# A float32 decoder block on one core: gate weights loaded into later tiles of the mixer, the row factor built a unit sooner, one opening cast behind the root

## The chip, the core and the metric

The kernel runs on one core of a Trainium2 chip. The engines of the core are called here as the profile calls them: PE (TensorE, matrix products), DVE (VectorE), ACT (ScalarE), POOL (GpSimd) and SP (SyncE, which issues nearly all DMA loads here). The metric is the device time of one execution in microseconds (us); a lower time is better.

## The reference

One layer of a decoder block on x of 256 tokens by 2048 columns, all in float32: a half-step feed-forward, a mixer of two head groups, a second half-step feed-forward, and a last norm.

```python
def rms_norm(x, gain):
    xf = x.astype(jnp.float32)
    var = jnp.mean(xf * xf, axis=-1, keepdims=True)
    return (xf * lax.rsqrt(var + NORM_EPS) * gain.astype(jnp.float32)).astype(x.dtype)

def swiglu_ffn(x, w_gate, w_up, w_down):
    return (jax.nn.silu(x @ w_gate) * (x @ w_up)) @ w_down
...
        x = x + FFN_RESIDUAL_SCALE * swiglu_ffn(rms_norm(x, ffn1_norm[l]),
                                                ffn1_w_gate[l], ffn1_w_up[l], ffn1_w_down[l])
        z = rms_norm(x, mix_norm[l]) @ w_in[l]
        ...
        xc = causal_depthwise_conv(lru_x, lru_conv_w[l]) + lru_conv_b[l]
        h = rg_lru(xc, lru_w_a[l], lru_b_a[l], lru_w_i[l], lru_b_i[l], lru_lambda[l])
        y_lru = h * jax.nn.gelu(lru_gate, approximate=True)
        y_sc = sc_b * causal_depthwise_conv(sc_c * sc_x, sc_conv_w[l])
        y = jnp.concatenate([rms_norm(y_lru, lru_out_norm[l]),
                             rms_norm(y_sc, sc_out_norm[l])], axis=-1)
        x = x + y @ w_out[l]
```

The feed-forward is 5632 wide, `w_in` has 5120 columns, and the gates of `rg_lru` are eight blocks of 128 by 128 in `lru_w_a` and in `lru_w_i`.

## The kernel before

**Products in parts.** A float32 operand is split into a high part `hi` (a cast on ACT) and a rest `lo` (a subtraction on DVE), and a product is made of hi by hi, lo by hi and hi by lo. Weights come in units of 512 rows by 512 columns (1 MB, a tile `raw_...`). `load` (line 165) issues the DMA on SP, `parts_of` makes two ACT casts of 128x1024 and one DVE subtraction of 128x2048. The pool `raws` has three raw buffers, which are used in turn: a load can go out when the subtraction has let go of the buffer three units back. The pool `splits` has two hi and two lo buffers; a cast waits until PE has left the unit two back. Every engine, and SP's queue too, works in order. Nearly all instructions are recorded through one helper, so they carry its line, 43.

**The mixer.** `columns` multiplies w_in, 512 columns at a time, in four units (u = 0 to 3) into four banks `ps_in`: per unit 16 matmuls with hi (512 columns wide) and 16 with lo (256 wide). A bank is one of eight of the PSUM pool. The normed x is turned into `xT_nm`, a tile for each unit, without the row factor 1/sqrt(mean of squares); that is multiplied in afterwards. `Norm.factor` makes it from the sums of squares (tiles `tot`, `v`, `s`, `y`, `q`, `r`), and `Norm.rows` spreads it: two diagonal tiles on DVE, two matmuls with ones into the bank `pb_nm`, and a DVE copy to `bc_nm`. The list `order` runs ten blocks of columns; the first two are `lru_x`. Behind the first block stand the row factor, then `gate_weights`, called twice: it loads the eight gate blocks (512 KB) into a buffer of `raws` (`rawgate_a`, `rawgate_i`), casts them and subtracts. In the names of the first block's tiles, `in_0_2` is unit 2 of block 0 and `in_1_0` unit 0 of the second block. `lru_x` then adds the two halves of each bank, multiplies by `bc_nm` to `zx`, and leaves the convolution (`xc`), its split (`xs`) and the gate products (`pgate_a`, `pgate_i`) to be issued between later units.

**Tiles of the mixer.** `tmp` takes tiles by tag from the pool `mixw`. The tags `d` and `v` have one buffer each of 128x1024. Their first user is the end of the first block's recurrence, many units later. The pool stands where the first feed-forward had its `keep` tiles, the last of which hold the crossed columns `cross_nm`; ACT reads those last.

**The opening.** `begin` is written out by hand and keeps its order (`Engine.pinned`). It multiplies the first units of the gate and up weights while x still arrives in four column groups (`load_x`). On ACT: two quarters of the up unit's cast at once (`hi_u_start`), the third quarter, the last square of the norm (`junk_n`), the root (`s_n`), the fourth quarter, then the tokens `n`. On DVE the chain from the sum `tot_n` over the root to `r_n`, then `lo_u_start`, the scaling of `ps_g`, and so on. `root`, made at the very start, loads the table for the square root.

A scheduler orders the instructions that are not pinned, so the order on each engine is read from the built program below.

Of the kernel before, what the change touches and what calls it, by code (L numbers as in the profile page):

```python
# [10 lines left out]
F32 = mybir.dt.float32  # L11
# [6 lines left out]
P = 128  # L18
D = 2048
# [5 lines left out]
CW = 512  # L25
NC_D = D // CW
UK = 4
NH = 8
# [21 lines left out]
def hybrid_block(ctx: ExitStack, tc: tile.TileContext, a: dict, out: bass.AP):  # L50
    nc = tc.nc
    Engine.pinned = False
    dve, act, pe = (Engine(tc, e) for e in (nc.vector, nc.scalar, nc.tensor))
# [6 lines left out]
    def defer(cost, fn):  # L60
        pending.append((cost, fn))

    def flush():
        while pending:
            pending.popleft()[1]()

    def pump(budget):

        owed[0] = min(owed[0], 0.0) + budget
        while pending and owed[0] > 0:  # L70
            cost, fn = pending.popleft()
            fn()
            owed[0] -= cost
# [5 lines left out]
    raws = ctx.enter_context(tc.tile_pool(name="raws", bufs=3, side="right"))  # L79
# [3 lines left out]
    def bank(name):  # L83
        return psum.tile([P, 512], F32, tag="ps", name=name)

    def f32(ap):
        return ap.bitcast(F32)
# [62 lines left out]
    def big(name):  # L150

        return bigs.tile([P, UK, 2 * S], F32R, tag="big", name=name)
# [39 lines left out]
    def unit(src, name):  # L192
        return parts_of(load(src, name), name)
# [21 lines left out]
    def onward():  # L215

        if moving:
            two, _, fn = moving.popleft()
            fn(two)
        if tasks:  # L220
            key, begin, fn = tasks.popleft()
            moving.append((begin(), key, fn))

    def on_the_way():
        return {task[0] for task in tasks} | {entry[1] for entry in moving}
# [103 lines left out]

    def columns(w, c0, xT, name):
        ps = [bank(f"ps_{name}_{f}") for f in range(4)]
        for u in range(KD // UK):
            blk = unit(w[u * UK * P : (u + 1) * UK * P, c0 : c0 + CW], f"{name}_{u}")
            assert ("nm", u) not in on_the_way()
            for half in range(2):
                for j in range(UK):
                    x = xT[u][:, j, :]
                    for f in range(4):  # L340
                        wf = blk[j][half][:, f * P : (f + 1) * P]
                        if half == 0:
                            pe.matmul(ps[f], wf, x, start=u == 0 and j == 0, stop=False)
                        else:
                            end = u == KD // UK - 1 and j == UK - 1
                            pe.matmul(ps[f][:, :S], wf, x[:, :S], start=False, stop=end)
            onward()
            pump(1.5)
        return ps

    def product(w, c, us, y, name):
        ps = [bank(f"ps_{name}_{t}") for t in range(NT)]
        cs = slice(c * CW, (c + 1) * CW)
        for i, u in enumerate(us):
            blk = unit(w[u * UK * P : (u + 1) * UK * P, cs], f"{name}_{u}")
            multiply([(ps[t], stationary(y(u), t), i == 0, i == len(us) - 1) for t in range(NT)], blk)
            pump(1.5)
        return ps  # L360
# [110 lines left out]
    def ffn(tag, norm, after, opening=False):  # L471
        with (
# [67 lines left out]
            ps = {(m, t): bank(f"ps_{m}{tag}_0_{t}") for m in "gu" for t in range(NT)}  # L540
            ws = {"g": wg, "u": wu}

            def first_columns(m, u, **how):
                return load(ws[m][u * UK * P : (u + 1) * UK * P, :CW], f"{m}{tag}_0_{u}", **how)

            def begin():
# [4 lines left out]
                raw = {("g", 0): first_columns("g", 0, pieces=pieces)}  # L551
# [58 lines left out]
                units.extend(big(f"x{tag}_{u}") for u in range(4))  # L610
                ru, (hi, lo, blk) = raw["u", 0], splits_of("u_start")
                act.copy(hi[:, :2], ru[:, :2])
                act.copy(hi[:, 2:3], ru[:, 2:3])
                norm.squares(3, (dve, act), lambda: pair[:, 0])
                norm.factor()
                act.copy(hi[:, 3:], ru[:, 3:])
                dve.tensor_tensor(lo, ru, f32(hi), op=ALU.subtract)
                n = tokens(1)
                rows = [stationary(norm.xT[0], t) for t in range(NT)]
# [231 lines left out]
    nm = held["nm"]  # L851


    with tc.tile_pool(name="mixer", bufs=1) as mp, tc.tile_pool(name="mixw", bufs=2) as mw:
        wgate = {}

        def gate_weights(key, src):
            raw = raws.tile([P, NH, P], F32, tag="raw", name=f"rawgate_{key}")
            nc.sync.dma_start(raw, src.rearrange("h i j -> i h j"))
            both = bigs.tile([P, 2, NH, P], F32R, tag="big", name=f"gate_{key}")  # L860
            hi, lo = both[:, 0], both[:, 1]
            act.copy(hi, raw)
            dve.tensor_tensor(lo, raw, f32(hi), op=ALU.subtract)
            wgate[key] = (hi, lo)
# [4 lines left out]
        w_in = a["w_in"][0]  # L869
# [3 lines left out]
        def tmp(tag, name, w=S, dt=F32, bufs=2):  # L873
            return mw.tile([P, w], dt, tag=tag, name=f"{tag}_{name}", bufs=bufs)
# [61 lines left out]
        def finish(y, k, gain, grp, first):  # L936
            sq = tmp("ysq", k)
            act.activation(sq, y, AF.Square)
            ac = acc[:, grp, :]
            if first:  # L940
                dve.tensor_copy(ac, sq)
            else:
                dve.tensor_tensor(ac, ac, sq, op=ALU.add)
            hi, lo = yT[k // UK][:, k % UK, :S], yT[k // UK][:, k % UK, S:]
            act.activation(hi, y, AF.Copy, scale=gain)
            dve.scalar_tensor_tensor(lo, y, gain, f32(hi), op0=ALU.mult, op1=ALU.subtract)
# [73 lines left out]
        def sc_b(ps, half):  # L1020
            if any(4 * half + f not in ys for f in range(4)):
                flush()
            for f in range(4):
# [4 lines left out]
                dve.tensor_tensor(y, b, y, op=ALU.mult)  # L1028
                defer(0.8, lambda q=q, y=y: finish(y, NH + q, vec["sc_out_norm"][:, q : q + 1], 1, q == 0))

        order = [
            (lru_x, 0, 0), (lru_x, 0, 1), (sc_c, 3, 0), (lru_gate, 1, 0), (sc_x, 4, 0),
            (lru_gate, 1, 1), (sc_c, 3, 1), (sc_x, 4, 1), (sc_b, 2, 0), (sc_b, 2, 1),
        ]
        for i, (use, piece, half) in enumerate(order):
            ps = columns(w_in, piece * (D // 2) + half * CW, nm.xT, f"in_{piece}_{half}")
            if i == 0:
                flush()
                nm.factor()
                nm.rows(lambda name: tmp("half", name, bufs=4))  # L1040
                bc = nm.bc
                dve.tensor_tensor(bc2, bc, bc, op=ALU.mult)
                gate_weights("a", a["lru_w_a"][0])
                gate_weights("i", a["lru_w_i"][0])
                yT += [big(f"yT_{u}") for u in range(KD // UK)]
            use(ps, half)

# [4 lines left out]
        for c in range(NC_D):  # L1052
            cs = slice(c * CW, (c + 1) * CW)
            for g in range(2):
                if c == 0 and g == 1:
                    flush()
                ps = product(w_out, c, (2 * g, 2 * g + 1), yT.__getitem__, f"o{c}_{g}")
# [92 lines left out]
```

## Time and profile before

| | |
|---|---|
| median of 3 runs | 1722.84 us (1720.89 to 1723.07) |
| the profiled execution, whole | 1723.02 us |
| its span, first to last instruction | 1721.2 us |
| mean granted PE clock in the span | 0.997 |
| DMA, mean over the span | 208 GB/s |
| loads of w_in, each 1 MB, median to landing | 5.1 us |

The profile is of one execution, so sums are made against 1723.02. Busy time is summed for each engine; idle time of an engine other than the one that bounds costs nothing. PE's matmuls overlap in their records, so the time of a unit is read from start to start. The text of the next section names views: the page, the waits (who waited for whom), the chain of work that ended last, the timeline, the table by windows, and the DMA issues.

### The profile page before, as it was taken

To read this page: it belongs to the slowest core of one execution; us is meant where nothing else is said; L and a number is where in the kernel's file an instruction comes from. 1 tells how busy PE (TensorE), PEld (TensorE's weight loads), DVE (VectorE), ACT (ScalarE), POOL (GpSimd) and SP (SyncE) were. 2 spreads that over 40 slices of the span, in tenths; PEclk is the share of its full clock that TensorE was granted. 3 is DMA by queue.
4 is the path that set the end of the run, shared out by engine and by line. 5 is a ranking of instruction groups with operands and counts; after the bars stand their busy time and mean duration, and the time that the engine had idled before them with its cause. 6 is when DMAs were issued, how large, how long until landed. Compare 5 with 4: busy or idle time off the path is not lost.

```text
span 1721.2 us, 20206 instructions
## 1 busy us (share of the span) xinstructions
PE 1700.1 (99%) x7811; PEld 1413.6 (82%) x7811; DVE 1477.9 (86%) x1286; ACT 1166.3 (68%) x1481; POOL 6.9 (0%) x32
## 2 busy tenths in 40 slices
PE   8999999999999999999999999999999999999997
PEld 6888888888887887888888888888888888887886
DVE  7988999989889878687987679989989888889796
ACT  6767667676568678765765776786667675677864
POOL 1000000000000000000000000000000000000000
PEclk9999999999999999999999999999999999999999
DMA  8667567585567685746555674585677656566853
GB/s 296 204 212 207 195 220 217 198 280 178 180 215 226 213 250 144 236 155 207 174 191 179 218 262 153 198 268 195 208 218 225 208 192 223 196 214 202 249 192 122
DMA packets 233056, 357.91 MB, mean 208 GB/s; under 512 B 64772, under 2 KB 67200, under 8 KB 232832
## 3 DMA queue, kind: packets, MB, share of 16 engines
q1 hardware_dynamic: 232496, 355.50, 63.9%
q8 instruction: 61, 1.00, 0.2%
q10 hardware_dynamic: 144, 1.05, 0.2%
q14 instruction: 35, 0.29, 0.0%
q0 software_dynamic: 320, 0.07, 0.0%
HBM read 339.82 MB, written 2.10 MB: 199 GB/s over the span
## 4 chain that ended last, share of the span: by engine, by line
PE 88%; DVE 4%; ACT 3%; DMA 2%; issue 2%; SPq 0%; DVEq 0%; ACTq 0%
PE ps_d L43 13%; PE ps_in L43 12%; PE ps_u_a L43 8%; PE ps_g_a L43 8%; PE ps_u_c L43 6%; PE ps_g_c L43 6%; PE ps_o L43 5%; PE ps_d_a L43 5%; PE ps_g_d L43 4%; PE ps_u_d L43 3%; PE ps_g_e L43 3%; PE ps_u_e L43 3%; PE ps_d_c L43 3%; PE ps_d_d L43 2%; PE ps_u L43 2%
## 5 line engine op out<-in xcount | busy, mean ns | idle before, releaser
L43 DVE TENSOR_TENSOR lo_u_p<-raw_u,hi_u_p 128x2048 fp32r<-128x2048 f32 (+1 forms) x80 | 160.0, 2019 | 18.7 <-ACT hi_u_p L43 18.2
L43 ACT CAST hi_u_p<-raw_u 128x1024 fp32r<-128x1024 f32 x140 | 141.6, 1048 | 48.9 <-PE ps_u_a L43 14.7
L43 ACT CAST hi_g_p<-raw_g 128x1024 fp32r<-128x1024 f32 x132 | 133.9, 1047 | 59.2 <-DVE raw_g L43 24.2
L43 PE MATMUL ps_d<-hi_d,h 128*128 128x512 f32 x704 | 167.0, 389 | 0.0
L43 DVE TENSOR_TENSOR lo_g_p<-raw_g,hi_g_p 128x2048 fp32r<-128x2048 f32 (+1 forms) x75 | 151.2, 2031 | 17.3 <-ACT hi_g_p L43 16.8
L43 PE MATMUL ps_in<-xT_nm,hi_in 128*128 128x512 f32 x640 | 154.5, 393 | 2.7 <-DVE bc_nm L43 2.7
L43 PEld LDWEIGHTS ps_d<-hi_d,h 128*128 128x128 f32 x704 | 132.1, 188 | 27.4
L43 PEld LDWEIGHTS ps_in<-xT_nm,hi_in 128*128 128x128 f32 x640 | 118.0, 189 | 26.3 <-DVE bc_nm L43 3.2
L43 ACT CAST hi_d_p<-raw_d 128x1024 fp32r<-128x1024 f32 x84 | 86.1, 1048 | 68.1 <-DVE raw_d L43 24.4
L43 DVE TENSOR_TENSOR lo_d<-raw_d,hi_d 128x2048 fp32r<-128x2048 f32 x44 | 100.2, 2289 | 32.9 <-ACT hi_d L43 32.7
L43 DVE TENSOR_TENSOR lo_in<-raw_in,hi_in 128x2048 fp32r<-128x2048 f32 x40 | 91.4, 2286 | 34.5 <-ACT hi_in L43 33.1
L43 ACT CAST hi_in<-raw_in 128x1024 fp32r<-128x1024 f32 x80 | 80.1, 1046 | 59.4 <-PE ps_in L43 38.8
L43 ACT CAST hi_u_x<-raw_u 128x1024 fp32r<-128x1024 f32 x80 | 81.3, 1047 | 41.8 <-PE ps_u_c L43 28.8
L43 DVE TENSOR_TENSOR lo_d_p<-raw_d,hi_d_p 128x2048 fp32r<-128x2048 f32 (+1 forms) x48 | 96.5, 2020 | 12.3 <-ACT hi_d_p L43 12.0
L43 DVE TENSOR_TENSOR raw_u<-raw_u,raw_u 128x2048 f32<-128x2048 f32 (+1 forms) x50 | 92.3, 1862 | 11.6 <-DMA raw_u<-in_ffn_w_up_dram 11.0
L43 ACT CAST hi_d<-raw_d 128x1024 fp32r<-128x1024 f32 x88 | 88.9, 1045 | 18.9 <-PE ps_d_d L43 7.6
L43 ACT CAST hi_g_x<-raw_g 128x1024 fp32r<-128x1024 f32 x80 | 81.6, 1045 | 28.3 <-PE ps_g_c L43 11.5
L43 DVE TENSOR_TENSOR lo_g_x<-raw_g,hi_g_x 128x2048 fp32r<-128x2048 f32 x40 | 91.4, 2286 | 5.6 <-ACT hi_g_x L43 5.6
L43 DVE TENSOR_TENSOR lo_u_x<-raw_u,hi_u_x 128x2048 fp32r<-128x2048 f32 x40 | 91.4, 2284 | 1.9 <-ACT hi_u_x L43 1.7
L43 DVE TENSOR_TENSOR raw_g<-raw_g,raw_g 128x2048 f32<-128x2048 f32 (+1 forms) x46 | 85.0, 1867 | 6.3 <-DMA raw_g<-in_ffn_w_gate_dram 6.2
L43 PE MATMUL ps_d<-lo_d,h 128*128 128x512 f32 x352 | 87.3, 389 | 0.0
L43 PEld LDWEIGHTS ps_in<-xT_nm,lo_in 128*128 128x128 f32 x640 | 82.5, 192 | 3.2
(399 smaller groups left out, 3671.5 us busy)
## 6 DMA issues: line engine op xcount, KB each, us to landing
raw_d<-in_ffn_w_down_dram SPq DMA_DIRECT2D x88, 1024.0 KB, 5.6
raw_u<-in_ffn_w_up_dram SPq DMA_DIRECT2D x87, 1024.0 KB, 5.3
raw_g<-in_ffn_w_gate_dram SPq DMA_DIRECT2D x86, 1024.0 KB, 5.4
raw_in<-in_w_in_dram SPq DMA_DIRECT2D x40, 1024.0 KB, 5.1
raw_o<-in_w_out_dram SPq DMA_DIRECT2D x16, 1024.0 KB, 5.1
xres<-in_x_dram SPq DMA_DIRECT2D x4, 512.0 KB, 7.5
raw_u<-in_ffn_w_up_dram SPq DMA_DIRECT2D x2, 512.0 KB, 9.2
raw_g_first<-in_ffn_w_gate_dram SPq DMA_DIRECT2D x1, 1024.0 KB, 11.9
```

The costliest lines, as they stand in the source:

```text
L43: ins = getattr(self.engine, name)(*args, **kwargs)
```

## The change

The gate weights are loaded into the tiles `d` and `v` instead of raw buffers; the row factor is made behind unit 1 of the first block and spread behind unit 2, through a callback of `columns`; in the opening, the third quarter of the cast goes behind the root, next to the fourth.

```diff
-    def columns(w, c0, xT, name):
+    def columns(w, c0, xT, name, between=None):
...
             onward()
             pump(1.5)
+            if between:
+                between(u)
         return ps
...
                 act.copy(hi[:, :2], ru[:, :2])
-                act.copy(hi[:, 2:3], ru[:, 2:3])
                 norm.squares(3, (dve, act), lambda: pair[:, 0])
                 norm.factor()
-                act.copy(hi[:, 3:], ru[:, 3:])
+                for j in (2, 3):
+                    act.copy(hi[:, j : j + 1], ru[:, j : j + 1])
...
-        def gate_weights(key, src):
-            raw = raws.tile([P, NH, P], F32, tag="raw", name=f"rawgate_{key}")
+        def gate_weights(key, src, room):
+            raw = tmp(room, f"gate_{key}", NH * P, bufs=1).rearrange("p (h j) -> p h j", h=NH)
...
+        def row_factor(u):
+            if u == 1:
+                flush()
+                nm.factor()
+            elif u == 2:
+                nm.rows(lambda name: tmp("half", name, bufs=4))
+
...
-            ps = columns(w_in, piece * (D // 2) + half * CW, nm.xT, f"in_{piece}_{half}")
+            between = row_factor if i == 0 else None
+            ps = columns(w_in, piece * (D // 2) + half * CW, nm.xT, f"in_{piece}_{half}", between)
             if i == 0:
-                flush()
-                nm.factor()
-                nm.rows(lambda name: tmp("half", name, bufs=4))
                 bc = nm.bc
                 dve.tensor_tensor(bc2, bc, bc, op=ALU.mult)
-                gate_weights("a", a["lru_w_a"][0])
-                gate_weights("i", a["lru_w_i"][0])
+                gate_weights("a", a["lru_w_a"][0], "d")
+                gate_weights("i", a["lru_w_i"][0], "v")
```

**The loads, on SP.** The place is the first block of the mixer. The rows are the difference of the two programs' order on SP's queue; `raw_in_0_3` is unit 3 of the first block, `raw_in_1_0` unit 0 of the second, and the last number of a name is a counter.

```order
-L165 DMA raw_in_0_3_5266<-in_w_in_dram 128x4x512
-L859 DMA rawgate_a<-in_lru_w_a_dram 128x8x128
-L859 DMA rawgate_i<-in_lru_w_i_dram 128x8x128
+L165 DMA raw_in_0_3_5287<-in_w_in_dram 128x4x512
 L165 DMA raw_in_1_0_5371<-in_w_in_dram 128x4x512
+L861 DMA d_gate_a<-in_lru_w_a_dram 128x8x128
+L861 DMA v_gate_i<-in_lru_w_i_dram 128x8x128
 L165 DMA raw_in_1_1_5432<-in_w_in_dram 128x4x512
```

Unit 0 of the second block has moved ahead of both gate loads, which stand together now. Elsewhere on SP one load moved: in the opening, `raw_g_0_01` stands ahead of `raw_u_0_2` instead of behind it.

**The row factor, on DVE and PE.** On DVE, the difference around the copy `bc_nm` (`bc_5110` is its square; `half_x` and `zx` are the first work of `lru_x`).

```order
-L43 TENSOR_TENSOR gate_a<-rawgate_a,gate_a 128x1024
-L43 TENSOR_TENSOR lo_in_0_3_5269<-raw_in_0_3_5266,hi_in_0_3_5268 128x2048
-L43 TENSOR_TENSOR gate_i<-rawgate_i,gate_i 128x1024
+L43 TENSOR_TENSOR gate_a<-d_gate_a,gate_a 128x1024
+L43 TENSOR_TENSOR gate_i<-v_gate_i,gate_i 128x1024
+L43 TENSOR_TENSOR lo_in_0_3_5290<-raw_in_0_3_5287,hi_in_0_3_5289 128x2048
 L43 TENSOR_TENSOR lo_in_1_0_5374<-raw_in_1_0_5371,hi_in_1_0_5373 128x2048
+L43 COPY bc_nm<-pb_nm 128x256
+L43 TENSOR_TENSOR bc_5110<-bc_nm 128x256
 L43 TENSOR_TENSOR lo_in_1_1_5435<-raw_in_1_1_5432,hi_in_1_1_5434 128x2048
-L43 COPY bc_nm<-pb_nm 128x256
```

The copy and its square moved ahead of the split of unit 1 of the second block, and both gate splits now stand ahead of unit 3 of the first. ACT's casts of the gate weights moved in the same way. On PE, the rows around `pb_nm` in the program before:

```order
L43 MATMUL ps_in_0_0_2_5113<-xT_nm_3_5166,lo_in_0_0_3_5269 128x256
L43 MATMUL ps_in_0_0_3_5114<-xT_nm_3_5166,lo_in_0_0_3_5269 128x256
L43 MATMUL pb_nm_5318<-half_diag_nm_5319,ones_82 128x128 x2
L43 MATMUL ps_in_0_1_0_5367<-xT_nm_0_4826,hi_in_0_1_0_5373 128x512
L43 MATMUL ps_in_0_1_1_5368<-xT_nm_0_4826,hi_in_0_1_0_5373 128x512
L43 MATMUL ps_in_0_1_2_5369<-xT_nm_0_4826,hi_in_0_1_0_5373 128x512
```

and of the change:

```order
L43 MATMUL ps_in_0_0_2_5113<-xT_nm_2_5087,lo_in_0_0_2_5243 128x256
L43 MATMUL ps_in_0_0_3_5114<-xT_nm_2_5087,lo_in_0_0_2_5243 128x256
L43 MATMUL pb_nm_5279<-half_diag_nm_5280,ones_82 128x128 x2
L43 MATMUL ps_in_0_0_0_5111<-xT_nm_3_5166,hi_in_0_0_3_5289 128x512
L43 MATMUL ps_in_0_0_1_5112<-xT_nm_3_5166,hi_in_0_0_3_5289 128x512
```

`pb_nm` moved from behind unit 3 of the first block to ahead of it. In both programs the second block's fourth bank (`ps_in_0_1_3`) is the one that `bc_nm` lets go. Before, PE's order left that bank's matmuls to the end of the unit's first half; in the change the first of them is the unit's fourth matmul.

**The opening, on ACT.** The difference between the first half of the up unit's cast and the tokens.

```order
 L43 CAST hi_u_start<-raw_u_0_0_128 128x1024
-L43 CAST hi_u_start<-raw_u_0_0_128 128x512
-L43 ACTIVATE junk_n_3_1_206,ss_n_111<-xres 128x512
-L43 ACTIVATE s_n_211<-v_n_210 128x2
-L43 CAST hi_u_start<-raw_u_0_0_128 128x512
-L43 ACTIVATE n_1_0_223<-xres,r_n_214 128x512
-L43 ACTIVATE n_1_1_224<-xres,r_n_214 128x512
+L43 ACTIVATE junk_n_3_1_205,ss_n_111<-xres 128x512
+L43 ACTIVATE s_n_210<-v_n_209 128x2
+L43 CAST hi_u_start<-raw_u_0_0_128 128x512 x2
+L43 ACTIVATE n_1_0_223<-xres,r_n_213 128x512
+L43 ACTIVATE n_1_1_224<-xres,r_n_213 128x512
```

The third quarter's cast moved from ahead of the last square to behind the root, where the fourth quarter's already stood.

## The prediction

> **What bounds the kernel.** First the page: TensorE's share, and the chain of work that ended last.
>
> ```profile
> PE 1700.1 (99%) x7811; PEld 1413.6 (82%) x7811; DVE 1477.9 (86%) x1286; ACT 1166.3 (68%) x1481; POOL 6.9 (0%) x32
> PE 88%; DVE 4%; ACT 3%; DMA 2%; issue 2%; SPq 0%; DVEq 0%; ACTq 0%
> ```
>
> TensorE (PE) is busy almost throughout and carries 88% of the chain. A change that removes no matmul can therefore gain only where PE stands still or runs slowly. The view of waits, for PE alone, lists where it stood (us in total, times, longest us):
>
> ```profile
> PE ps_in L43 <- DVE bc_nm L43: 2.7, 1, 2.7
> ...
> PE ps_u L43 <- ACT hi_u_start L43: 0.6, 1, 0.6
> PE pt L43 <- ACT n L43: 0.3, 1, 0.3
> PE ps_g L43 <- DVE x L43: 0.3, 1, 0.3
> ```
>
> The first lies in the mixer, behind the copy `bc_nm` of the row factor; the other three lie in the first 36 us. The change edits both places. PE's timeline around the mixer's wait (start, length, engine, line, operation):
>
> ```profile
> 714.28 3.82 PE L43 MATMUL ps_in<-xT_nm,hi_in 128*128 128x512 f32 x16
> ...
> 719.85 3.82 PE L43 MATMUL ps_in<-xT_nm,hi_in 128*128 128x512 f32 x16
> ...
> 725.42 0.60 PE L43 MATMUL pb_nm<-half_diag_nm,ones 128*128 128x128 f32 x4
> 725.78 2.78 PE L43 MATMUL ps_in<-xT_nm,hi_in 128*128 128x512 f32 x11
> 731.29 2.50 PE L43 MATMUL ps_in<-xT_nm,hi_in 128*128 128x512 f32 x5 [2.73 <-DVE bc_nm L43]
> ...
> 735.74 2.46 PE L43 MATMUL ps_in<-xT_nm,hi_in 128*128 128x512 f32 x10
> ```
>
> One unit of the projection (16 long and 16 short matmuls) takes 719.85 - 714.28 = 5.57 us from start to start. The unit that starts at 725.78 takes 735.74 - 725.78 = 9.96 us. So this place loses **4.39 us**, not 2.73. The rest is the clock, which the table by windows shows (PEclk is the third number from the end):
>
> ```profile
> 719.85:725.42 5.57, 5.57 (x35) 4.92 (x34) 2.03 (x2) 1.99 (x2) 0.00 (x0) 1.00 1.00 360
> 731.29:735.74 4.45, 4.45 (x21) 3.97 (x22) 4.02 (x12) 2.47 (x4) 0.00 (x0) 0.68 0.73 241
> ```
>
> After the wait the granted clock is 0.68 over 4.45 us, and 4.39 - 2.73 = 1.66 us goes there. [...]
>
> Why the copy is late is in the chain of work and on SP's queue:
>
> ```profile
> 719.43 7.05 DMA raw_in<-in_w_in_dram
> ...
> 726.58 2.00 ACT hi_in L43 x2
> 728.61 2.29 DVE lo_in L43
> 730.90 0.35 DVE bc_nm L43
> ```
> ```profile
> 703.58 0.37 SPq L859 DMA_DIRECT2D rawgate_a<-in_lru_w_a_dram  x1
> 714.52 0.37 SPq L859 DMA_DIRECT2D rawgate_i<-in_lru_w_i_dram  x1
> 717.23 46.11 SPq L165 DMA_DIRECT2D raw_in<-in_w_in_dram  x10
> ```
>
> The copy stands on VectorE (DVE) behind the split `lo_in_1_1`, that behind its cast, that behind a load issued at 719.43. The load is so late because the two gate loads hold two of the three raw buffers: at 703.58 a buffer came free, and `rawgate_a` took it instead of `raw_in_1_0`, which went out only at 717.23.
>
> **The change, mixer.** No work is added; instructions move.
>
> *Loads.* On SP `raw_in_1_0` takes the place at 703.58. The gate loads follow into tiles of the mixer's pool, whose memory the feed-forward's tiles used last. They must wait for the last reader there, ScalarE's (ACT) two joins of `cross_nm`:
>
> ```profile
> 702.52 2.57 ACT L43 COPY pair<-cross_nm 128x1024 uint16<-128x1024 uint16 x2 [1.30 <-DMA cross_nm<-pair]
> ...
> 713.52 1.06 ACT L43 CAST gate_a<-rawgate_a 128x1024 fp32r<-128x1024 f32 x1
> ```
> ```profile
> 717.12 2.29 DVE L43 TENSOR_TENSOR lo_in<-raw_in,hi_in 128x2048 fp32r<-128x2048 f32 x1
> ```
> ```profile
> DMA to landing us min/median/max: 5.0/5.2/8.1
> ```
>
> That is 705.09, so they go out at 705.1 and 705.5. With the landings of `raw_in` between 690 and 745 us (last row) they are there between 710 and 713.6. ACT reaches the first gate cast at 713.52: no wait. Queued behind them on SP is only `raw_in_1_1`, whose buffer comes free at 714.5 anyway (the release that let `rawgate_i` go); it lands by 722.6 at the latest, before PE and ACT want it (below).
>
> *Casts.* Both gate casts now stand ahead of `hi_in_0_3` on ACT, so it starts 1.06 us later, at 715.5 instead of 714.46, and ends by 717.6; PE comes to it at 719.85 + 0.36 (the moved `pb_nm`) = 720.21. On DVE the second gate split delays `lo_in_0_3` the same way: 717.12 + 1.2 + 2.29 = 720.6, needed 3.65 us after 720.21. Both delays are covered, by 2.6 and 3.2 us; beyond that each us would cost one.
>
> *Row factor.* `pb_nm` moves from 725.42 to 719.85: the same 0.36 us, elsewhere. DVE now has `lo_in_1_0` after `lo_in_0_3` (its data landed long before, its cast can end near 720.2 once PE is off the old buffer), so 720.6 + 2.29 = 722.9, then the copy, done by 723.3. PE's first matmul into the bank that the copy frees comes about three matmuls after 725.78: margin 3 us. The 2.73 us and the slow clock behind them go: 4.39 us.
>
> *What is late next.* With PE 4.4 us earlier, the candidate is the first gate matmul, which wants the cast `xs`:
>
> ```profile
> 736.77 0.39 ACT L43 CAST xs<-xc 128x256 fp32r<-128x256 f32 x1
> ```
> ```profile
> 738.04 0.28 PE L43 MATMUL pgate_a<-xs,gate_a 128*128 128x256 f32 x1
> ```
>
> Before, `xs` was ready at 737.16, 0.88 us ahead. `lo_in_1_1` will end at 724.1 + 2.0 + 2.29 = 728.4 instead of 730.9 (its cast now waits for PE to leave a buffer near 724.1, no longer for DMA), 2.5 us earlier. If the path from there to `xs` keeps its length, `xs` comes at 734.6 and PE, at 738.04 - 4.39 = 733.65, waits 1.0. But `bc_nm` leaves that path, and so does its square, of the same shape: twice 0.35 us, which leaves a wait of 0.3. That `xc` on ACT now also comes ahead of a weight cast can only shorten it. Ends 0 and 1.0; I take 0.3, the count in which all that is known to leave is left out. Mixer: 0.3 - 4.39 = **-4.1 us**.
>
> **The change, opening.** PE and ACT there:
>
> ```profile
> 14.56 2.91 PE L43 MATMUL ps_u<-hi_u_start,xT_n 128*128 128x512 f32 x12
> 18.03 1.20 PE L43 MATMUL ps_u<-hi_u_start,xT_n 128*128 128x512 f32 x4 [0.56 <-ACT hi_u_start L43]
> ...
> 22.51 3.80 PE L43 MATMUL ps_g<-hi_g_next,x 128*128 128x512 f32 x16
> ...
> 35.86 3.68 PE L43 MATMUL ps_g<-hi_g,x 128*128 128x512 f32 x15 [0.28 <-DVE x L43]
> ```
> ```profile
> 15.59 0.62 ACT L43 CAST hi_u_start<-raw_u 128x512 fp32r<-128x512 f32 x1 [1.66 <-DMA raw_u<-in_ffn_w_up_dram]
> 16.12 0.63 ACT L43 ACTIVATE junk_n<-xres 128x512 f32<-128x512 f32 x1
> ...
> 17.27 0.20 ACT L43 ACTIVATE s_n<-v_n 128x2 f32<-128x2 f32 x1 [0.43 <-DVE v_n L43]
> 17.38 0.60 ACT L43 CAST hi_u_start<-raw_u 128x512 fp32r<-128x512 f32 x1
> 18.29 1.34 ACT L43 ACTIVATE n<-xres,r_n 128x512 f32<-128x512 f32 x2 [0.31 <-DVE r_n L43]
> ```
> ```profile
> 14.31 0.69 DVE L43 SCALAR_TENSOR_TENSOR pair<-xres 128x512 f32<-128x512 f32 x1
> ...
> 16.87 0.16 DVE L43 TENSOR_REDUCE tot_n<-ss_n 128x2 f32<-128x8 f32 x1 [1.86 <-ACT junk_n L43]
> ...
> 18.21 2.29 DVE L43 TENSOR_TENSOR lo_u_start<-raw_u,hi_u_start 128x2048 fp32r<-128x2048 f32 x1
> ```
>
> ACT sat 1.66 us waiting for the second half of `raw_u`, with the last square queued behind, although its input was there (DVE squares the same columns at 14.31). Now the square runs at 14.3, `tot_n` at 15.05, the root 0.40 later as before, done at 15.65; that is when the weights land (15.57), so the third quarter's cast keeps its time (15.6 to 16.2), and the fourth follows at once, done at 16.7 instead of 17.98. PE's wait of 0.56 goes, since its twelfth matmul ends at 17.47. `lo_u_start` starts at 16.74 instead of 18.21: 1.47 us earlier, and DVE is then occupied back to back until PE's wait at 35.86 in the chain of waits. Can the next load keep up?
>
> ```profile
> raw_g<-in_ffn_w_gate_dram SPq DMA_DIRECT2D x1, 1024.0 KB, 11.7
> ```
>
> This one (issued at 6.57, us to landing last) is there at 18.3, before ACT needs it for `hi_g_next` after the tokens `n`, at about 18.0: 0.3 us, inside ACT's slack. One more load is moved: `raw_g_0_01` goes ahead of `raw_u_0_2` on SP. Nothing wants the latter for several units; cost taken as 0, bounds 0 and 0.3. The gain lies between the three short waits (0.6 + 0.3 + 0.3 = 1.2) and DVE's 1.47; I take **-1.4 us**, since the chain runs over DVE.
>
> **Sum.** -4.1 - 1.4 = -5.5 us. The profiled execution took 1723.02 us (span 1721.2, about 1.8 around it; nothing there changes), so 1717.5. The median of the three runs, 1722.84, lies 0.18 lower; against it this is -0.3%. A measurement of this kernel can tell about 0.2%, 3.4 us, from no change.
>
> **Rivals.**
>
> - [...] Chance 0.10.
> - *Opening without gain.* The last columns of x land nearly as late as the weights, and both casts now stand behind the root; then -4.1 alone: 1718.9. The square at 14.31 speaks against it. Chance 0.13.
> - *A new wait in the mixer*: `xs` is late by more than 1.0 and the clock falls again (2.7 in all, of which 0.3 is in the sum): 1717.5 + 2.4 = 1719.9. The 0.88 us of slack before speak for a small one only. Chance 0.08.
> - *Slower: gate loads hold ACT.* The casts are in order: should `v_gate_i` land at L, `hi_in_0_3` ends at L + 1.05 + 2.02 and PE waits from L = 717.1 on, one us for one, plus 1.66 for the clock. It turns the sign from L = 721; at 723 it costs 5.9 + 1.7 and gives 1725.1. It would take a landing 17 us after issue where the rows say 8.1 at most. Chance 0.03.
> - *No effect* (loads and copies fall where they fell): the order of both programs differs at just these places, so 1723, chance 0.04.
>
> **Chances.** Forecast 0.62. Faster by over 0.2% (below 1719.4): forecast, opening rival and part of the first, less some for the runs' spread (1720.89 to 1723.07): 0.77. Slower 0.03, the rest 0.20. Range: from the uncut sum (4.39 + 1.47 gives 1717.2) less 1.6 for that spread, to past the third rival: 1715.6 to 1720.6.
>
> **What would show it.** Right: no PE wait on `bc_nm`, granted clock 1.00 through the second block's first unit, that unit near 5.6 us; `raw_in_1_0` issued near 703.6 less the opening's gain; PE's x16 on `hi_g_next` near 21.0 instead of 22.51. Wrong: PE waiting for `hi_in`, `lo_in` or `xs` there, ACT idle ahead of a gate cast, or ACT waiting for `xres` ahead of the last square.

## The result

The changed kernel takes 1716.79 us (median of 7 runs, 1716.44 to 1717.24); the kernel before took 1722.18 us beside it (7 runs, 1720.87 to 1723.07). The ratio is 0.9967, with a 95% interval of 0.9957 to 0.9976: 5.4 us, or 0.33%, less. The profiled execution took 1716.68 us (span 1714.9, against 1721.2).

The page of the changed kernel, TensorE's share and the chain of work that ended last:

```profile
PE 1698.0 (99%) x7811; PEld 1413.0 (82%) x7811; DVE 1478.5 (86%) x1286; ACT 1166.9 (68%) x1481; POOL 6.9 (0%) x32
PE 91%; DVE 4%; ACT 2%; issue 2%; DMA 1%; SPq 0%; DVEq 0%; ACTq 0%
```

The counts are those of before: no work was added. PE's share of the chain rose from 88 to 91%. The view of waits for PE, the list behind its first two rows, which are waits for x and for the norm's weights at the start:

```profile
PE ps_g_c L43 <- DVE lo_g_p L43: 1.1, 4, 0.3
PE ps_g L43 <- DVE x L43: 0.3, 1, 0.3
PE ps_d_c L43 <- ACT s_d L43: 0.3, 1, 0.3
```

`ps_in <- bc_nm` (2.7) is gone, and so are two of the opening's three short waits. PE's timeline at the places that the prediction speaks of:

```profile
14.89 3.79 PE L43 MATMUL ps_u<-hi_u_start,xT_n 128*128 128x512 f32 x16
...
21.27 3.79 PE L43 MATMUL ps_g<-hi_g_next,x 128*128 128x512 f32 x16
...
717.87 0.60 PE L43 MATMUL pb_nm<-half_diag_nm,ones 128*128 128x128 f32 x4
718.23 3.92 PE L43 MATMUL ps_in<-xT_nm,hi_in 128*128 128x512 f32 x16
...
723.90 3.82 PE L43 MATMUL ps_in<-xT_nm,hi_in 128*128 128x512 f32 x16
...
729.47 2.46 PE L43 MATMUL ps_in<-xT_nm,hi_in 128*128 128x512 f32 x10
731.77 0.28 PE L43 MATMUL pgate_a<-xs,gate_a 128*128 128x256 f32 x1
```

The first unit of the second block takes 729.47 - 723.90 = 5.57 us, where it took 9.96. The difference, 4.39 us, is the whole loss that was read from the profile of before. By windows, the same unit (granted clock third from the end):

```profile
723.90:729.47 5.57, 5.57 (x35) 4.92 (x34) 5.26 (x10) 3.25 (x8) 0.00 (x0) 1.00 0.64 210
```

Set beside before, PE's starts give the whole sum. `ps_g <- hi_g_next` is 1.24 us earlier (22.51 to 21.27). PE then keeps a lead of about 1.2 us through the first feed-forward. At `ps_d_a`, near its end, the lead becomes 1.97, because a wait of 0.59 for `u_d` that stood there before is absent. The unit that begins at 725.78 in before begins at 723.90, a lead of 1.88, and the next one (735.74, now 729.47) has a lead of 6.27. So the opening gives 1.2, a step that nobody edited 0.75, the mixer 4.39. The opening's and the mixer's part are tried below by edits, the step by a second profile.

### The profile page after: what moved, and what is told of

Read it like the earlier page. It is cut to its first block, busy times and chain, and to the rows that moved or that the text cites. A ratio compares the mean times of both kernels' runs of the same rounds, so it can differ in the third digit from the quotient of the medians.

```text
span 1714.9 us, 20207 instructions
## 1 busy us (share of the span) xinstructions
PE 1698.0 (99%) x7811; PEld 1413.0 (82%) x7811; DVE 1478.5 (86%) x1286; ACT 1166.9 (68%) x1481; POOL 6.9 (0%) x32
## 4 chain that ended last, share of the span: by engine, by line
PE 91%; DVE 4%; ACT 2%; issue 2%; DMA 1%; SPq 0%; DVEq 0%; ACTq 0%
PE ps_d L43 14%; PE ps_in L43 13%; PE ps_u_a L43 9%; PE ps_g_a L43 8%; PE ps_u_c L43 6%; PE ps_g_c L43 6%; PE ps_o L43 5%; PE ps_d_a L43 5%; PE ps_g_d L43 4%; PE ps_u_d L43 3%; PE ps_g_e L43 3%; PE ps_u_e L43 3%; PE ps_d_c L43 3%; PE ps_d_d L43 2%; PE ps_u L43 2%; PE ps_g L43 2%
```

## The experiments

All medians stand beside runs of the kernel before on the same chip; these had medians of 1721.9 (the first four kernels), 1722.43 (the two repeats, gate_i four times, and the scalings of x), 1722.73 (both mixer edits and the changed kernel again, gate_i five times) and 1722.78 us (the last one).

**The opening's edit alone.**

```diff
-                act.copy(hi[:, 2:3], ru[:, 2:3])
                 norm.squares(3, (dve, act), lambda: pair[:, 0])
                 norm.factor()
-                act.copy(hi[:, 3:], ru[:, 3:])
+                for j in (2, 3):
+                    act.copy(hi[:, j : j + 1], ru[:, j : j + 1])
```

> The kernel before with the opening's cast alone moved. Theory: the last square and the root leave the wait for the second half of raw_u, so PE reaches the matmuls on hi_g_next about 1.2 us sooner (as in the profile of the change, 22.51 to 21.27) and keeps it: 1.2 us below before, about 1721.0 against 1722.2; the wait for bc_nm in the mixer (2.7 us) and the slow clock behind it stay. The profile of the change also gained 0.75 us at the end of the first feed-forward, where a wait of 0.6 for the copy u_d went. Rival 1: that step belongs to the opening too (everything in front of the mixer stands 1.2 us sooner against some transfer), then 2.0 us in all and no wait for u_d here. Rival 2: it is chance in one execution, then the wait for u_d comes and goes between profiles of one program.

Measured: 1720.78 us (1719.02 to 1722.28), ratio 0.9994 [0.9985, 1.0003]. The interval takes in 1, so this run alone does not show the gain at the end; a closer pair follows below. The trace shows `hi_g_next` at 21.23. It also shows something that the expectation has wrong: the wait on `bc_nm` is 1.60 us, not 2.7, and the clock does not fall. Timeline, then the window behind the wait:

```profile
724.57 2.78 PE L43 MATMUL ps_in<-xT_nm,hi_in 128*128 128x512 f32 x11
728.95 1.42 PE L43 MATMUL ps_in<-xT_nm,hi_in 128*128 128x512 f32 x5 [1.60 <-DVE bc_nm L43]
...
732.12 2.46 PE L43 MATMUL ps_in<-xT_nm,hi_in 128*128 128x512 f32 x10
```
```profile
728.70:732.10 3.40, 3.15 (x21) 2.93 (x22) 3.40 (x11) 2.11 (x4) 0.00 (x0) 1.00 1.04 369
```

The unit loses 732.12 - 724.57 - 5.57 = 1.98 us here, 0.38 more than the wait, although the clock is at 1.00. So the mixer's loss is not a constant of the kernel before; the repeats below follow this up. The step at `ps_d_a` was the other question: the wait for `u_d` is in this trace too, with 0.7 us, so the opening's edit does not remove it.

**The loads alone** (gate weights into `d` and `v`; the row factor stays).

```diff
-            raw = raws.tile([P, NH, P], F32, tag="raw", name=f"rawgate_{key}")
+            raw = tmp(room, f"gate_{key}", NH * P, bufs=1).rearrange("p (h j) -> p h j", h=NH)
```

> The kernel before with the gate weights alone moved into the tiles d and v; the row factor stays behind the block, so bc_nm still stands on DVE behind lo_in_1_1. Theory: the loads are the cause. raw_in_1_0 and raw_in_1_1 go out when they did not wait for gate buffers, lo_in_1_1 ends near 728.0 on before's clock, bc_nm near 728.4, and PE comes to the freed bank at about 728.3: the wait shrinks from 2.7 us to 0.0 to 0.3, the clock stays at 1.00, and 4.1 to 4.4 us go: about 1718.0 against 1722.2. Rival: the place of bc_nm in the order is the cause; then the wait stays near 2.7 us and the time does not move.

Measured: 1717.98 us (1717.78 to 1719.06), ratio 0.9979 [0.9970, 0.9987]: 3.9 us less. PE's timeline has no wait on `bc_nm`:

```profile
725.80 4.06 PE L43 MATMUL ps_in<-xT_nm,hi_in 128*128 128x512 f32 x16
729.70 2.07 PE L43 MATMUL ps_in<-xT_nm,lo_in 128*128 128x256 f32 x16
731.61 2.46 PE L43 MATMUL ps_in<-xT_nm,hi_in 128*128 128x512 f32 x10
```

The unit takes 5.81 us, 0.24 more than a free one. The copy, still behind `lo_in_1_1`, ends at 728.39 by DVE's timeline; in this program's order the unit's twelfth matmul is the first that needs the bank, some 2.5 us after 725.80, so PE all but meets it. By this unit the edit carries 4.15 of the 4.39 us.

**The row factor alone** (built behind unit 1, spread behind unit 2; the loads stay).

```diff
+            if between:
+                between(u)
...
+        def row_factor(u):
+            if u == 1:
+                flush()
+                nm.factor()
+            elif u == 2:
+                nm.rows(lambda name: tmp("half", name, bufs=4))
```

> The kernel before with the row factor alone moved a unit sooner; the gate weights still hold raw buffers. On DVE bc_nm now stands ahead of lo_in_1_0. Theory (late loads): the wait for bc_nm goes, but raw_in_1_1 still lands at 726.5 and lo_in_1_1 still ends at 730.9, with the half sums, zx, xc and xs behind it, so xs is ready near 736.1 while PE wants it at 733.65: a new wait of about 2.4 us ahead of pgate_a, and the clock falls again if so long a wait lowers it: 0.3 to 2.0 us below before, 1720.2 to 1721.9. Rival (place in the order): no wait is left, 4.4 us go, 1717.8.

Measured: 1721.65 us (1720.62 to 1723.34), ratio 1.0001 [0.9992, 1.0010]. The time is not told apart from the kernel before. The wait on `bc_nm` goes, and another takes its place. PE's timeline, and the windows of that unit and of the stretch behind the wait:

```profile
735.13 0.39 PE L43 MATMUL pgate_a<-xs,gate_a 128*128 128x256 f32 x1 [2.01 <-ACT xs L43]
```
```profile
725.10:730.67 5.57, 5.57 (x34) 4.92 (x33) 4.15 (x6) 3.08 (x6) 0.00 (x0) 1.00 0.82 272
```
```profile
735.13:739.37 4.24, 4.24 (x17) 3.66 (x18) 4.14 (x6) 1.35 (x3) 0.10 (x1) 0.60 0.22 36
```

With the copy out of the way, PE runs on to the first gate product. There `xs` is late, because the load behind it all (`raw_in_1_1`) is as late as before: it was issued at 718.63 and took 6.95 us, with PE 0.7 us earlier than in the profile of before (719.43 and 7.05), and ACT starts its cast at 725.68 after a wait of 2.05 for it. The split behind it, on DVE, waits for its cast:

```profile
727.71 2.29 DVE L43 TENSOR_TENSOR lo_in<-raw_in,hi_in 128x2048 fp32r<-128x2048 f32 x1 [1.42 <-ACT hi_in L43]
```

Behind the wait of 2.01 the granted clock falls (0.60 over 4.24 us) as behind that of 2.73 (0.68 over 4.45). The late load is the cause, and the place of the wait only the symptom.

**Both edits of the mixer, without the opening's; then the same beside the changed kernel.** The diff is that of the change without the lines in `begin`.

> Both mixer edits without the opening's. Theory: no wait for bc_nm or xs, granted clock 1.00 there, the unit that took 9.96 us takes 5.57: 4.4 us below before, 1717.8 against 1722.2, and the change less the opening's 1.2. If the step of 0.75 us at the end of the first feed-forward belongs to the opening, the wait for u_d (0.6) is here; if it is chance, it may be or not. Rival (the slow clock is not the wait's): 0.5 stays granted for some 3 us near there and 2.7 us go, 1719.5.

> Both edits of the mixer without the opening's, once more, now beside the changed kernel on the same chip, so that the difference of the two is the opening's edit alone. Theory (the opening gives 1.2 us): 1718.0, that is 1.2 above the changed kernel. Rival (the opening gains nothing that lasts and the earlier difference was between sessions): within 0.3 of the changed kernel.

> The changed kernel, unaltered, beside the mixer's edits alone: theory 1716.8 and 1.2 below that kernel; rival, within 0.3 of it. In its trace the wait ps_d_a <- ACT u_d may be there or not (0 to 0.7 us), since its length depends on when cross_nm lands; if it is, the whole run is that much longer.

Measured: 1718.0 us (1717.15 to 1719.08), ratio 0.9978 [0.9969, 0.9986] the first time. The second time 1718.42 (1717.92 to 1719.40) beside 1717.35 (1716.99 to 1717.66) for the changed kernel. No run of the one reaches the other's range, so the opening's edit is worth about 1.1 us at the end. The loads alone had 1717.98 in the same session as 1718.0 here: by the medians, the row factor's edit adds nothing that can be seen once the load is early. In the first of these traces the unit takes 731.21 - 725.64 = 5.57 us and `pgate_a` does not wait:

```profile
725.64 3.82 PE L43 MATMUL ps_in<-xT_nm,hi_in 128*128 128x512 f32 x16
729.30 2.08 PE L43 MATMUL ps_in<-xT_nm,lo_in 128*128 128x256 f32 x16
731.21 2.46 PE L43 MATMUL ps_in<-xT_nm,hi_in 128*128 128x512 f32 x10
733.50 0.28 PE L43 MATMUL pgate_a<-xs,gate_a 128*128 128x256 f32 x1
```

The repeat of the changed kernel bears on the step at `ps_d_a`: its list of PE's waits has the wait that the first profile of the same program lacked.

```profile
PE ps_d_a L43 <- ACT u_d L43: 0.6, 1, 0.6
```

So the wait comes and goes between executions of the changed kernel. Of the fourteen traces of this study eight have it, with 0.4 to 0.7 us, four with the old order of the opening and four with the new. The 0.75 us that no edit explained can therefore not be counted as a gain of the change. All three traces of the kernel before have the wait; what decides over it is not shown.

**The kernel before, twice more**, and **the opening's edit, once more.**

> The kernel before once more, for the spread between executions of one program. Theory (the short waits depend on when loads land): the PE wait on bc_nm comes back with another length than 2.73 us, between about 1.6 (as in the opening-only kernel, where raw_in_1_1 landed sooner) and 2.8; the wait ps_d_a <- ACT u_d comes back anywhere from 0 to 0.7 us. The granted clock falls for one interval of about 3.4 us where the wait is 2.0 us or more and stays at 1.00 where it is 1.6 or less. Rival (the program alone sets them): 2.7 and 0.6 again in each execution, with the slow interval.

> As for the first repeat of the kernel before: theory, a bc_nm wait between 1.6 and 2.8 us and a u_d wait between 0 and 0.7 us, other than in the first repeat by more than 0.1 us in at least one of them; rival, 2.7 and 0.6 both times.

> The opening's edit alone, once more. Its first profile showed a bc_nm wait of 1.6 us without a fall of the clock, and its times lay in two groups (1719.0 to 1719.9 and 1720.8 to 1722.3). Theory (the wait on bc_nm has another length in each execution, and the clock falls behind the longer ones): two groups again, over 1 us apart; the profiled execution is near 1722 if its wait is 2.0 us or more, with a granted clock near 0.5 for 3.4 us behind it, and near 1720 or less if its wait is 1.6 or less. Rival (the opening's shift itself shortens the wait): 1.6 us again and clock 1.00, and times within 1 us of 1719.5.

Measured: 1722.96 and 1724.50 us for the two executions; 1721.18 us (1718.89 to 1722.53), ratio 0.9990 [0.9981, 0.9999], for the opening's edit. The times of the latter spread over 3.6 us rather than fall into two clear groups. In the traces, the chain of work of the first and of the second repeat, up to PE's wait, and PE's timeline there:

```profile
719.43 6.80 DMA raw_in<-in_w_in_dram
```
```profile
731.04 1.96 PE L43 MATMUL ps_in<-xT_nm,hi_in 128*128 128x512 f32 x5 [2.49 <-DVE bc_nm L43]
```
```profile
719.58 7.47 DMA raw_in<-in_w_in_dram
...
727.15 2.00 ACT hi_in L43 x2
...
729.17 2.29 DVE lo_in L43
731.47 0.35 DVE bc_nm L43
```
```profile
731.86 2.50 PE L43 MATMUL ps_in<-xT_nm,hi_in 128*128 128x512 f32 x5 [3.10 <-DVE bc_nm L43]
```

The wait of the second repeat, 3.10, lies above the range that was expected; the wait for `u_d` came back with 0.5 and 0.6. The wait on `bc_nm` follows the landing of one load. Over three executions of one program that load took 7.47, 7.05 and 6.80 us, and PE waited 3.10, 2.73 and 2.49. With the opening's edit it took 5.96 the first time and 6.19 the second, and PE waited 1.60 and 1.94 (the chains of both):

```profile
718.18 5.96 DMA raw_in<-in_w_in_dram
```
```profile
717.91 6.19 DMA raw_in<-in_w_in_dram
```

The wait of 1.94 was followed by a slow stretch:

```profile
728.90 1.43 PE L43 MATMUL ps_in<-xT_nm,hi_in 128*128 128x512 f32 x5 [1.94 <-DVE bc_nm L43]
```
```profile
730.00:733.40 3.40, 3.40 (x18) 3.35 (x17) 3.40 (x11) 3.40 (x5) 0.00 (x0) 0.54 0.87 304
```

The rival, that the opening's shift itself sets 1.6 and keeps the clock up, is refuted by this row; that the shift makes the load land somewhat sooner is not excluded by two executions.

**The cast and the subtraction of gate_i done four times, then five times**, in the changed kernel.

```diff
-            act.copy(hi, raw)
-            dve.tensor_tensor(lo, raw, f32(hi), op=ALU.subtract)
+            for _ in range(4 if key == "i" else 1):
+                act.copy(hi, raw)
+                dve.tensor_tensor(lo, raw, f32(hi), op=ALU.subtract)
```

> The changed kernel, with the cast and the subtraction of gate_i done four times (same result each time). In program order the extra work stands behind unit 3 of the first block: on DVE two subtractions ahead of the copy bc_nm and one ahead of lo_in_1_1, on ACT the casts around hi_in_1_0 and ahead of hi_in_1_1. Theory (DVE's path from lo_in_1_1 over half_x, zx and xc to xs is what stands 0.2 us ahead of PE at pgate_a): following the rows, bc_nm is copied near 722.1 instead of 720.7 and costs nothing, lo_in_1_1 starts near 726.3 instead of 724.2, xs is ready near 733.7 instead of 731.6, and PE waits 1.9 us for xs at pgate_a (1.5 to 2.3). If a wait of this length lowers the clock, as 2.0 us did with the factor alone, 1.7 more goes with it: +1.9 to +3.6 us against the changed kernel's 1716.8, so 1718.7 to 1720.4. Rival (the extra work lies beside PE and ACT's idle 4 us at 718 to 722 takes it up): no wait, 1716.8.

> As the kernel with gate_i done four times, with a fifth: one more subtraction (1.2 us) stands on DVE between lo_in_1_1 and half_x, so xs comes 1.1 to 1.7 us later and PE waits 2.6 to 3.2 us at pgate_a instead of 1.5. Theory (how long PE stands decides over the clock, 1.6 does not lower it and 2.0 does): the granted clock falls to about 0.5 for one interval of some 3.4 us behind this wait and costs 1.7 us: 2.6 to 3.2 and 1.7 over the changed kernel's 1716.8, so 1721.1 to 1721.7 without a wait at u_d. Rival (the fall belongs to that stretch of the kernel before, not to the length): the clock stays at 1.00, 1719.4 to 1720.0.

Measured, four times: 1719.03 us (1718.07 to 1719.62), ratio 0.9980 [0.9971, 0.9989]. DVE's timeline, then PE's:

```profile
725.68 1.22 DVE L43 TENSOR_TENSOR gate_i<-v_gate_i,gate_i 128x1024 fp32r<-128x1024 f32 x1
726.82 2.28 DVE L43 TENSOR_TENSOR lo_in<-raw_in,hi_in 128x2048 fp32r<-128x2048 f32 x1
```
```profile
734.24 0.38 PE L43 MATMUL pgate_a<-xs,gate_a 128*128 128x256 f32 x1 [1.53 <-ACT xs L43]
```

PE reached this place 0.8 us later than in the first profile of the changed kernel. Beside it the copy `bc_nm` (at 722.81, 2.1 later) lost 1.3 and cost nothing; `lo_in_1_1` (2.6 later) lost 1.8, and PE waited 1.53 at `pgate_a`, at the low end of what was expected. DVE's path from `lo_in_1_1` to `xs` is therefore next to bind, and its slack is a few tenths of a us.

Five times: 1719.13 us (1718.04 to 1719.71), ratio 0.9979 [0.9970, 0.9988], and a wait of 1.46 instead of 2.6 to 3.2. The expectation failed for a reason of its own: it counted on the old order, but in this program fifteen instead of ten matmuls of the unit stand ahead of `pgate_a`, and those covered the extra time.

```profile
729.42 3.59 PE L43 MATMUL ps_in<-xT_nm,hi_in 128*128 128x512 f32 x15
734.47 0.39 PE L43 MATMUL pgate_a<-xs,gate_a 128*128 128x256 f32 x1 [1.46 <-ACT xs L43]
```

So this run does not tell the length of a wait apart from its place; the second run of the opening's edit does, since there the same place went both ways.

**The opening's two scalings of x behind the low part of unit 2**, in the changed kernel: the attempt at a better version.

```diff
-                plain(1, units[1])
-                plain(0, units[0])
...
+                plain(1, units[1])
+                plain(0, units[0])
```

> The changed kernel, with the opening's two scalings of x (plain 1 and plain 0) issued on DVE and ACT behind the low part of unit 2 of the up weights instead of ahead of the gate's parts; meant to remove the remaining PE wait ps_g <- DVE x (0.3 us, at 34.65). Theory (DVE sets the pace there): the wait goes and with it 0.3 us, at most 0.5: 1716.3 to 1716.5, below what the interval can tell; the x15 on ps_g starts near 34.3 in the trace. Rival (what was ahead of DVE's low part now holds ACT's cast for unit 2): PE waits for hi_u instead, and the time stays within 0.3 of 1716.8 or rises to 1717.3.

Measured: 1717.25 us (1716.85 to 1718.24), ratio 0.9970 [0.9958, 0.9981]. The wait for `x` is gone from PE's timeline:

```profile
34.12 3.79 PE L43 MATMUL ps_g<-hi_g,x 128*128 128x512 f32 x16
```

This execution starts `hi_g_next` 0.14 us later than the first profile of the changed kernel and is 0.05 ahead of it at the unit that starts at 46.29, so some 0.2 of the expected 0.3 us is there. But PE's list of waits has a new 0.3 for `hi_g_p` later on, and the median lies between the changed kernel's two, 1716.79 and 1717.35. No gain is shown, and the changed kernel stays the fastest that was run.

## Why the prediction was right

The forecast, faster by 5.5 us, was right, and by the mechanisms that it named. Point by point:

- *Loads.* Between the two profiles SP's times shift by the 1.97 us that PE is ahead there, so the predicted 705.1 and 705.5 should read 703.1 and 703.5. SP's timeline of the changed kernel:

```profile
699.53 2.42 SPq L165 DMA_DIRECT2D raw_in<-in_w_in_dram  x2
703.16 0.37 SPq L861 DMA_DIRECT2D d_gate_a<-in_lru_w_a_dram  x1
703.58 0.59 SPq L861 DMA_DIRECT2D v_gate_i<-in_lru_w_i_dram  x1
```

  The first line ends with `raw_in_1_0`, out at about 701.6 (that is 703.6 less 1.97). The gate loads took 7.4 and 8.6 us to land, the second longer than the 8.1 that the prediction held for the most in that stretch. It was there at 712.2, 0.3 us before ACT came free for it:

```profile
711.56 1.06 ACT L43 CAST gate_a<-d_gate_a 128x1024 fp32r<-128x1024 f32 x1
712.50 1.07 ACT L43 CAST gate_i<-v_gate_i 128x1024 fp32r<-128x1024 f32 x1
713.45 2.02 ACT L43 CAST hi_in<-raw_in 128x1024 fp32r<-128x1024 f32 x2
```

- *Casts.* No wait: the second gate load was those 0.3 us early, and behind it stands a slack. `hi_in_0_3` ends at 715.47, 2.76 us before PE starts on it at 718.23; 2.6 were predicted.
- *Row factor.* DVE's timeline has the copy at 720.70, and PE needs the bank about three matmuls after 723.90: margin 3.5 us, 3 predicted.
- *What is late next.* This is the term that was off: 0.3 us was charged for `xs`, bounds 0 and 1.0, and 0 was measured. DVE's and ACT's timelines:

```profile
724.21 2.29 DVE L43 TENSOR_TENSOR lo_in<-raw_in,hi_in 128x2048 fp32r<-128x2048 f32 x1 [2.63 <-ACT hi_in L43]
```
```profile
731.18 0.80 ACT L43 CAST xs<-xc 128x256 fp32r<-128x256 f32 x2
```

  `lo_in_1_1` ends at 726.50, which with the lead of 1.88 is the predicted 728.4. From there to the first `xs` it is 731.58 - 726.50 = 5.08 us, where the count in the prediction left 6.26 - 0.70 = 5.56. The rest, 0.48, is close to what the prediction named without a price, `xc` ahead of a weight cast: before, DVE stood 0.43 us in this path for an `xc` of ACT, and in the changed kernel it does not. The slack is 0.2 us, so the candidate was the right one. Mixer: -4.39 measured, -4.1 predicted.
- *Opening.* In the pair of profiles 1.24 us, predicted 1.4. In all fourteen traces of this study, `hi_g_next` starts at 22.51 to 22.79 with the old order (seven, mean 22.68) and at 21.14 to 21.41 with the new one (seven, mean 21.26). The means differ by 1.4 us; the first profile of before has the earliest of the old ones. With the new order ACT waits 0.36 to 0.39 us for `xres` ahead of the last square in all seven, here in the first profile of the changed kernel:

```profile
14.51 0.63 ACT L43 ACTIVATE junk_n<-xres 128x512 f32<-128x512 f32 x1 [0.36 <-DMA xres<-in_x_dram]
```

  The prediction named such a wait as a sign against the forecast. It is small: the square starts at 14.51 instead of 14.3, and `lo_u_start` at 16.99 instead of 16.74. Over the fourteen traces the mean gain at this place is the predicted one all the same; of it, about 1.1 us is left in the time of the whole.
- *Slow clock.* It went with the wait, as the forecast said: in the profile of the changed kernel the granted clock is 1.00 over 715 to 742 us. The split of the loss was rough: the prediction put all of 1.66 us down to the clock, but its own row of 0.68 over 4.45 us accounts for 0.32 x 4.45 = 1.42, and the opening alone lost 0.38 beside its wait at full clock. The sum does not hang on the split, since both parts go with the wait. In the eight executions of the table in the last section the clock fell behind the waits of 1.94 to 3.10 us and stayed at 1.00 behind those of 1.46 to 1.60. That it falls there without the wait, to which the first of the rivals' chances (0.10) belongs, no run shows.
- *The sum.* -4.39 - 1.24 gives -5.6 on the profiled execution; 6.34 were measured there, and the remaining 0.7 is the absent wait for `u_d`, which the same program shows in its repeat. The medians differ by 5.39. That this comes within 0.1 us of the forecast is in part luck: the loss of the mixer, read from one execution, was 4.39 there and 1.98 to 6.0 in others with the same wait, and the opening was put 0.3 too high against the time of the whole, as the mixer was put 0.3 too low. The median itself, 1716.79, lies 0.7 below the forecast 1717.5.

The factor alone shows what a count of that edit by itself would have missed: its gain lies wholly behind the load, and is 0.24 us by one trace (5.81 less 5.57), and nothing by the medians, once the load is early.

## What to carry to other kernels

Follow a wait back to the transfer at the head of its chain before moving the instruction that it names: moving the copy alone only moved the wait to the next consumer (2.01 us at `pgate_a`), and freeing the buffer for the load removed 4.15 of the 4.39 us. Read a loss from unit start to unit start, since the named wait can be little more than half of it (3.10 of 6.0 us in the second repeat of before). Compare two programs over several executions of each: one trace of each put 0.75 us where no edit was.

## What the hardware showed beside this

Read in steps of 0.1 us, the granted clock fell from 1.00 to 0.50 at no fixed distance from the wait: at 730.7 in the profile of before, within PE's wait, at 731.7 in its first repeat, 0.7 us after PE had resumed, and at 730.26 in the second run of the opening's edit, 1.35 us after. It was back at 1.00 after 3.4 us in four executions and after 6.8 in one:

| kernel | wait, us | slow stretch, us |
|---|---|---|
| before | 2.73 | 3.4 |
| before, first repeat | 2.49 | 3.4 |
| before, second repeat | 3.10 | 6.8 |
| row factor alone | 2.01 | 3.4 |
| opening alone, second | 1.94 | 3.4 |
| opening alone, first | 1.60 | none |
| gate_i four times | 1.53 | none |
| gate_i five times | 1.46 | none |

The length of the wait sorts the eight (none fell at 1.60 and less, all at 1.94 and more); what sets off the fall, and what ends it, is not shown. The first 10 us are left aside: there the column prints 1.00, although matmuls of 512 columns start 0.42 us apart in the profile of before (8.66 to 9.08) and 0.23 later (10.90 to 11.13). The second repeat stayed slow for 6.8 us, and PE stood for the first 1.2 of them (730.7 to 731.86):

```profile
731.00:734.40 3.40, 2.54 (x7) 2.06 (x8) 3.40 (x11) 0.60 (x1) 0.00 (x0) 0.50 0.71 220
734.40:737.80 3.40, 3.40 (x18) 3.35 (x18) 2.48 (x7) 3.29 (x5) 0.10 (x1) 0.54 0.46 180
```

It lost 737.56 - 725.98 - 5.57 = 6.0 us to a wait of 3.10. So the load's landing decides how long PE stands (5.96 to 7.47 us of transfer, 1.60 to 3.10 us of waiting); beside the wait the unit loses 0.4 us where the clock stays up (the opening alone), and 1.7 to 2.9 us where it falls. This fits the spread of the times: the kernel before takes 1719.36 to 1723.72 us in 33 runs of one session, the changed kernel 1716.44 to 1717.24 in 7. The wait is not all of the spread, since both edits of the mixer without the opening's, which have no such wait in their traces, spread over 1.9 us in 11 runs.
